# A gate convolution in PSUM, operands in small steps, one tile in another pool and a last column set after loading: several edits to a hybrid transformer block

## The chip, the cores and the metric

The kernel runs on one core of one Trainium2 chip. Its engines are TensorE (PE, matrix products), VectorE (DVE), ScalarE (ACT), GpSimd (POOL) and SyncE (SP, which here only issues loads); each works through its own queue in order. The metric is the device time of one execution, in microseconds (us); lower is better.

## The reference

A block of a generator over 2048 tokens of width 1024 (and 256 context tokens) is computed in fp32. After three kinds of heads (neighbourhood attention, a gating MLP, a convolution module) come an output projection, a residual, and the part that matters here, a gated MLP with a centred depthwise convolution of three tokens on its gate, 2816 channels wide:

```python
x = x + gate1 * (mix @ w_out)                      # output projection, residual
h = modulate(rmsnorm(x), shift2, scale2)           # mean square over the 1024 channels
g, u = split(h @ w_up)                             # gate and up, 2816 each
a = silu(dwconv3(g, ffn_conv_w, ffn_conv_b)) * u   # over tokens t-1, t, t+1
x = x + gate2 * (a @ w_down)
out = rmsnorm(x)
```

## The kernel before, in words

Tokens are kept in four blocks of 512 (0 to 3), a tile is 128 channels x 512 tokens. PE multiplies with fp32 split in two: ACT writes a high half (a copy rounded to fp32r), then DVE or POOL writes the low half, source minus high half; three matmuls take the place of one. `halves` and `split_comb` do that for operands, `load_w` for the weights of the projections. Which engine writes the low half of a weight is set by `phase(i)` out of the list `CFG` ("V" DVE, "P" POOL, "PV" both in turn).

**Output projection.** `out_tile(b, f, w)` makes tile f of block b: it loads the old x (`xr`), 24 matmuls go to a PSUM bank `po`, DVE adds the residual (L859, tile `x1`), the result is stored to DRAM as `x1d`, and its squares are summed over f into `accs[b]`, by DVE for blocks 2 and 3 (L310). For block 2 the sum lives in the pool `jp`, in a tile that an earlier stage used; for block 3 it is `ssum_last`. `out_stats` turns a block's sum into the factor `r`, stored as `rsd`.

**Up stage.** The product with `w_up` is done as a 2 x 2 block matrix product with seven products instead of eight: rows are the two halves of the channels, columns two token blocks. Token half t=0 is blocks 0 and 1, t=1 blocks 2 and 3. The seven operands of a half are sums of four tiles b11, b12, b21, b22: T1 = b12 - b11, T2 = b22 - T1, T3 = b22 - b12, T4 = b21 - T2, and B11, B21, B22 as they are. `h2_tile` loads one tile from `x1d`, scales (DVE, L1117) and shifts it (ACT). For t=0 the operands are made at the end of the output projection: `first_half` runs as a second lane in `merge` beside `out_proj`, `first_half_rest` after it; they stay in SBUF in `hcomb`. For t=1 they are made during t=0 by the generator `second_half` and stored to DRAM (`td`), to be read back by `reload`. Each call `next(sh)` performs the code up to the next `yield`.

For each of 11 pairs k, `up_pair(t, k)` calls `winograd` twice, for the gate tiles and the up tiles: seven `up_prod` of 12 matmuls each into the PSUM tiles x, y, z, and sums that DVE makes out of them (L1274 to L1284). The gate goes to `gb` (one buffer), the convolution over it is ACT for the first tap (L1307), DVE for two more (L1309), ACT for silu (L1311), for four tiles; then the products with u (L1314, L1319), the seven combinations for the down stage (POOL) and their stores to `actd`. PE names are `g_5x` (pair 5, gate, PSUM tile x) and `u_5x`.

**Last column.** Pairs of t=0 lack the gate's right neighbour of their last token, which only t=1 has. After t=1, `last_column` computes that column, and it is written into the DRAM tensors `actd[0]` of five products. **Down stage.** `product` loads two tiles at a time (`ra`), splits them (`ah`), builds the weights' halves (`dw`) and multiplies (L1451).

The order of instructions on an engine is set by the planner: by the order of the code, by `merge` and `weave` (lanes weighed by their cost in us), by `high_priority`, and by when pool memory comes free: with `reuse_waits="tile"` a tile waits for whatever last used its addresses.

Of the kernel before, what the change touches and what calls it, by code (L numbers as in the profile page):

```python
# [143 lines left out]
def tile_hybrid_block(ctx: ExitStack, tc: tile.TileContext, a, out):  # L144
# [69 lines left out]
    CFG = "V,P;PV,P;PV,P;PV,P".split(";")  # L214
# [916 lines left out]
    def first_half():  # L1131
# [6 lines left out]
        for kk in range(4):  # L1138
# [12 lines left out]
    def first_half_rest():  # L1151
        for kk in range(4):
            split_comb(B21, kk, held[B21, kk], nc.vector)
        for kk in range(4):
# [2 lines left out]
            nc.gpsimd.tensor_tensor(t2, hh[:, kk, :].bitcast(F32), hl[:, kk, :].bitcast(F32), op=ALU.add)
# [109 lines left out]
    def winograd(w, c12, c21, c22, use_c11, name):  # L1267
# [16 lines left out]
        nc.vector.tensor_tensor(c12, c12, z, op=ALU.add)  # L1284

    def up_pair(t, k, wg, wu):
        nm = f"{t}_{k}"
# [16 lines left out]
        for i, l in ((0, 0), (1, 1), (1, 0), (0, 1)):
            f, o = k + NP * i, l * TB
            c = stp.tile([P, TB], F32, tag="c", bufs=6, name=f"c{nm}{i}{l}")
            nc.scalar.activation(c, gb[:, i, o:o + TB], AF.Identity, scale=fcw[:, f, 0:1], bias=fcw[:, f, 3:4])  # L1307
# [41 lines left out]
    for t in range(2):  # L1349
# [256 lines left out]
```

## Time and profile before

| | |
|---|---|
| median of 3 runs | 2421.2 us (2420.14 to 2424.05) |
| the profiled execution | 2424.5 us, span of its records 2422.6 us |
| mean granted PE clock | 0.974 |
| end of attention, start of output projection of blocks 2, 3 | near 975 us |
| up stage, t=0 | from about 1058 to 1505 us |
| up stage, t=1 | from 1505 to 1938 us |
| down stage | from 1938 us to the end |

Rows of a profile give an engine, a line of the kernel, an operation and "out<-in"; numbers of buffers are left out. "[8.89 <-ACT dw000hl L1096]" behind a row means that the engine had been idle for 8.89 us before it, until ACT's instruction of line 1096 that writes `dw000hl` had ended. A busy engine is not at its peak by that alone: the clock column says how fast PE was allowed to run, 1.00 being full speed.

### The profile page before, as it was taken

The page shows a single profiled execution, that of the slowest core. Times are in us where ns is not written, and L with a number is a line of the kernel's source. Part 1 is how long each engine was busy: PE and PEld are TensorE (multiplying, and loading weights), DVE is VectorE, ACT ScalarE, POOL GpSimd, SP SyncE. Part 2 cuts the span into 40 slices and gives each one's busy share as a digit, 9 for nine tenths or more (in the row PEclk, how much of TensorE's full clock was granted, in tenths as well). Part 3 has the DMA queues.
Part 4 walks back from the last instruction along what each step waited for, and adds up shares of the span by engine and source line. Part 5 has one row for each costly group of instructions (what it writes and reads, how often), then busy time and mean ns, then how long its engine had stood idle before and what let it go on. Part 6 is the DMA issues. An engine that isn't in the chain of part 4 may idle for free.

```text
span 2422.6 us, 34336 instructions
## 1 busy us (share of the span) xinstructions
PE 2288.3 (94%) x12452; PEld 1901.2 (78%) x12452; DVE 1841.5 (76%) x2477; ACT 1139.1 (47%) x1988; POOL 1097.0 (45%) x1008
## 2 busy tenths in 40 slices
PE   7999989999998999989999998999999989989996
PEld 5889778988887788768777786888888867868875
DVE  4785656556784974698798888787777768999997
ACT  4765643356565446454343434443443344344443
POOL 0265312012011222455667565556565468665753
PEclk9999999999999999989999999999999999999998
DMA  9675576658878778633334434633233492345322
GB/s 355 232 244 171 201 231 189 179 170 240 246 226 269 197 220 272 221 122 118 126 134 157 152 131 166 234 105 109 96 111 103 135 332 93 93 142 176 96 78 92
DMA packets 186347, 421.74 MB, mean 174 GB/s; under 512 B 27072, under 2 KB 76096, under 8 KB 184128
## 3 DMA queue, kind: packets, MB, share of 16 engines
q1 hardware_dynamic: 144688, 318.82, 42.2%
q0 software_dynamic: 28320, 94.39, 10.4%
q10 hardware_dynamic: 13168, 6.32, 0.9%
q8 instruction: 98, 1.61, 0.3%
q14 instruction: 73, 0.60, 0.1%
HBM read 311.69 MB, written 107.77 MB: 173 GB/s over the span
## 4 chain that ended last, share of the span: by engine, by line
PE 55%; DVE 16%; DMA 12%; issue 7%; ACT 5%; POOL 4%; SPq 1%; DVEq 0%; ACTq 0%; POOLq 0%
PE po L202 4%; PE pv L1451 3%; PE pu L1451 2%; PE pk L202 2%; DMA adaf<-in_ada 2%; PE p L1451 2%; PE obank L202 2%; PE pq L202 2%; PE tp L202 2%; PE s L202 2%; PE tp L208 2%; DMA bias_t<-in_bias 2%; DVE cv L573 1%; DMA kk<-ks 1%; DMA xb<-x1d 1%
## 5 line engine op out<-in xcount | busy, mean ns | idle before, releaser
L573 DVE SCALAR_TENSOR_TENSOR cv<-hconv,cst,cv 128x512 f32<-128x512 f32 x240 | 213.9, 933 | 12.3 <-ACT cv L567 12.2
L693 DVE CUSTOM_DVE_ANT_0 sb<-s,bias_t 128x544 f32<-128x544 f32 (+3 forms) x128 | 105.0, 821 | 107.7 <-PE s L202 82.6
L696 ACT ACTIVATE sb<-sb,mx 128x544 f32<-128x544 f32 (+3 forms) x128 | 106.3, 831 | 167.7 <-DVE mx L693 163.2
L1309 DVE SCALAR_TENSOR_TENSOR c<-gb,cst,c 128x512 f32<-128x512 f32 x176 | 166.1, 968 | 3.1 <-ACT c L1307 2.8
L1096 ACT ACTIVATE ah<-ra 128x512 fp32r<-128x512 f32 x154 | 95.0, 623 | 119.8 <-PE pu L1451 32.6
L1097 POOL TENSOR_TENSOR ah<-ra,ah 128x512 fp32r<-128x512 f32 x72 | 112.0, 1569 | 69.4 <-ACT ah L1096 69.4
L202 PE MATMUL s<-kk,qq 128*128 128x256 f32 (+4 forms) x512 | 103.6, 325 | 14.5 <-DMA kk<-ks 8.4
L202 PEld LDWEIGHTS s<-kk,qq 128*128 128x128 f32 x512 | 89.4, 193 | 34.0 <-issue 12.5
L208 PE MATMUL tp<-cst,sb 128*128 128x128 f32 (+2 forms) x672 | 98.4, 277 | 11.4 <-DVE pt L728 7.6
L208 PEld LDWEIGHTS tp<-cst,sb 128*128 128x128 f32 (+2 forms) x672 | 80.6, 140 | 31.2 <-DVE pt L728 8.9
L1097 DVE TENSOR_TENSOR ah<-ra,ah 128x512 fp32r<-128x512 f32 x82 | 84.3, 1030 | 19.0 <-ACT ah L1096 19.0
L1307 ACT ACTIVATE c<-gb,cst 128x512 f32<-128x512 f32 x88 | 69.0, 809 | 27.7 <-DVE gb L1282 26.2
L962 POOL TENSOR_TENSOR adaf<-adaf,adaf 128x1024 f32<-128x1024 f32 x16 | 40.9, 2559 | 89.7 <-ACT adaf L959 89.7
L1311 ACT ACTIVATE c<-c 128x512 f32<-128x512 f32 x88 | 55.3, 629 | 52.5 <-DVE c L1309 52.2
L726 ACT ACTIVATE pt<-tp 128x384 f32<-128x384 f32 (+2 forms) x128 | 61.2, 478 | 36.3 <-PE tp L208 35.9
L728 DVE COPY pt<-tp 128x256 f32<-128x256 f32 (+1 forms) x128 | 57.7, 450 | 24.5 <-PE tp L208 24.2
L959 ACT ACTIVATE adaf<-adaf,silu_c 128x256 f32<-128x256 f32 x128 | 54.3, 498 | 43.2 <-DMA adaf<-in_ada 42.6
L196 POOL DMA_DIRECT2D actd<-c x66 | 36.5, 553 | 80.6 <-DVE c L1319 64.2
L196 POOL DMA_DIRECT2D x1d<-x x30 | 16.6, 553 | 117.3 <-DVE x L859 89.3
L196 POOL DMA_DIRECT2D ks<-k x60 | 33.5, 561 | 77.7 <-ACT k L226 47.5
L196 POOL DMA_DIRECT2D mixd<-att x14 | 7.7, 550 | 134.2 <-DVE att L227 130.3
L202 PE MATMUL obank<-pt,vt 128*64 128x128 f32 (+2 forms) x832 | 58.4, 277 | 0.2 <-DVE pt L728 0.2
(2410 smaller groups left out, 8022.3 us busy)
## 6 DMA issues: line engine op xcount, KB each, us to landing
ra<-actd SPq DMA_DIRECT2D x70, 512.0 KB
wg<-in_w_up SPq DMA_DIRECT2D x44, 512.0 KB
wu<-in_w_up SPq DMA_DIRECT2D x44, 512.0 KB
actd<-tt POOLq DMA_DIRECT2D x88, 256.0 KB, 2.4
actd<-c POOLq DMA_DIRECT2D x66, 256.0 KB, 2.4
adaf<-in_ada SPq DMA_DIRECT2D x32, 512.0 KB
qq<-qs SPq DMA_DIRECT2D x64, 256.0 KB
adaf<-in_ada SPq DMA_DIRECT2D x8, 1024.0 KB
```

What stands on the lines that cost most here:

```text
L196: st_eng[0].dma_start(plain(dst), plain(src))
L202: x = nc.tensor.matmul(*args, **kw)
L208: x = nc.tensor.transpose(*args)
L573: nc.vector.scalar_tensor_tensor(acc[ct], hb[:, ct, k:k + TB], cvw[:, ct, k:k + 1], acc[ct], op0=ALU.mult, op1=ALU.add)
L693: x = nc.vector.tensor_tensor_reduce(out=sb[:, w], in0=s[:, w], in1=bt[:, w], scale=-1.0, scalar=3.0e38, op0=ALU.add, op1=ALU.min, accum_o ...
L696: nc.scalar.activation(sb[:, w], sb[:, w], AF.Exp, bias=mx, scale=-1.0, accum_out=rs[:, cb, j:j + 1])
L726: nc.scalar.activation(dst, src, AF.Copy)
L1096: nc.scalar.activation(hl[:, 0, :], src, AF.Copy)
L1097: eng.tensor_tensor(hl[:, 1, :], src, hl[:, 0, :].bitcast(F32), op=ALU.subtract)
L1307: nc.scalar.activation(c, gb[:, i, o:o + TB], AF.Identity, scale=fcw[:, f, 0:1], bias=fcw[:, f, 3:4])
L1309: nc.vector.scalar_tensor_tensor(c, gb[:, i, o + d:o + d + TB], fcw[:, f, d:d + 1], c, op0=ALU.mult, op1=ALU.add)
L1451: nc.tensor.matmul(ps[i], w[:, ww, sl], ah[:, aa, :], start=start and k_ == 0 and m == 0, stop=(k_ == NP - 1 and m == 2), skip_group_check ...
```

## The change

Six edits.

1. `phase(2)` with "V,P" is set ahead of the last `merge`, so DVE alone writes the low halves of the last projection weights (six of them go from POOL to DVE).
2. The sum of squares of block 2 (`ssum_2`) lies in the pool `pair` instead of `jp`.
3. In `first_half` and `first_half_rest` the low halves of B11 and B22 and the additions `td` go from POOL to DVE (12 operations of 128x512).
4. `second_half` makes its operands in seven steps for each kk, with all subtractions and splits on DVE (8 splits were POOL's), and is called by `step` at two places of each `winograd` of t=0 from the second pair on; `run_all(sh)` performs what is left.
5. For t=0 the first tap and the first DVE tap of the convolution go to a PSUM tile (`cs`, one buffer, tag "st"), the second DVE tap reads it and writes `c` in SBUF.
6. The five DMAs of the last column go; instead ACT copies the column into each loaded `ra` tile of the five products (30 copies of 128x2 or 128x1) ahead of the split.

```diff
-    CFG = "V,P;PV,P;PV,P;PV,P".split(";")
+    CFG = "V,P;PV,P;V,P".split(";")
...
+        elif b == 2 and f == 0:
+            pair("skip")
+            accs[b] = pairp.tile([P, 2, TB], F32, tag="pair", name="ssum_2")[:, 0, :]
+            nc.scalar.activation(accs[b], x1, AF.Square)
...
-                split_comb(p, kk, x, nc.gpsimd if p == B11 else nc.vector)
+                split_comb(p, kk, x, nc.vector)
...
-            nc.gpsimd.tensor_tensor(t2, hh[:, kk, :].bitcast(F32), hl[:, kk, :].bitcast(F32), op=ALU.add)
+            nc.vector.tensor_tensor(t2, hh[:, kk, :].bitcast(F32), hl[:, kk, :].bitcast(F32), op=ALU.add)
...
-            split_comb(B22, kk, h2_tile(0, kk, 1, 1, held["rs"], "xe"), nc.gpsimd)
+            split_comb(B22, kk, h2_tile(0, kk, 1, 1, held["rs"], "xe"), nc.vector)
...
+    phase(2)
...
+        def out_(p, kk, x, eng):
+            if p in SPLIT:
+                x = halves(x, fws, "sp", 3, f"tbs{kk}{p}", eng)
+            store(td[p][:, kk], x)
+
+        def less(kk, x, y, n):
+            t = tt(f"tb{kk}{n}")
+            nc.vector.tensor_tensor(t, x, y, op=ALU.subtract)
+            return t
+
         for kk in range(4):
-            xs = []
-            for i in range(2):
-                xs += [h2_tile(1, kk, i, l, rs, "xb") for l in range(2)]
-                yield
-            cs = combine(*xs, f"tb{kk}", nc.vector)
-            for p in range(7):
-                c = cs[p]
-                if p in SPLIT:
-                    c = halves(c, fws, "sp", 3, f"tbs{kk}{p}", nc.vector if p < 3 else nc.gpsimd)
-                store(td[p][:, kk], c)
-                if p == 3:
-                    yield
+            b11, b12 = (tile(kk, 0, l) for l in range(2))
+            yield
+            t1 = less(kk, b12, b11, 0)
+            store(td[B11][:, kk], b11)
+            b22 = tile(kk, 1, 1)
+            yield
+            out_(T1, kk, t1, nc.vector)
+            t3 = less(kk, b22, b12, 2)
+            yield
+            t2 = less(kk, b22, t1, 1)
+            store(td[B22][:, kk], b22)
+            out_(T3, kk, t3, nc.vector)
+            yield
+            b21 = tile(kk, 1, 0)
+            out_(T2, kk, t2, nc.vector)
+            yield
+            t4 = less(kk, b21, t2, 3)
+            store(td[B21][:, kk], b21)
+            yield
+            out_(T4, kk, t4, nc.vector)
             yield
...
         nc.vector.tensor_tensor(c22, c22, z, op=ALU.add)
+        step()
         up_prod(B21, x, w, False)
...
         nc.vector.tensor_tensor(c12, c12, z, op=ALU.add)
+        step()
...
+        def step():
+            if t == 0 and k > 0:
+                next(sh, None)
...
-        if t == 0:
-            next(sh, None)
...
-            nc.scalar.activation(c, gb[:, i, o:o + TB], AF.Identity, scale=fcw[:, f, 0:1], bias=fcw[:, f, 3:4])
-            for d in (1, 2):
-                nc.vector.scalar_tensor_tensor(c, gb[:, i, o + d:o + d + TB], fcw[:, f, d:d + 1], c,
+            ps = c if t else pp.tile([P, TB], F32, tag="st", bufs=1, name=f"cs{nm}{i}{l}")
+            nc.scalar.activation(ps, gb[:, i, o:o + TB], AF.Identity, scale=fcw[:, f, 0:1], bias=fcw[:, f, 3:4])
+            for d, to in ((1, ps), (2, c)):
+                nc.vector.scalar_tensor_tensor(to, gb[:, i, o + d:o + d + TB], fcw[:, f, d:d + 1], ps,
                                                op0=ALU.mult, op1=ALU.add)
...
-        for p, v in ((T2, t2), (T1, t1), (T3, t3), (T4, b12), (B22, b22)):
-            nc.scalar.dma_start(actd[0][p][:, :, TB - 1:], v.unsqueeze(2))
+        lastc.update({T2: t2, T1: t1, T3: t3, T4: b12, B22: b22})
...
-            if t == 0 and k > 0:
-                next(sh, None)
         if t == 0:
+            run_all(sh)
             reload()
...
+                        if t == 0 and p in lastc:
+                            nc.scalar.activation(at[:, 0:n, TB - 1:], lastc[p][:, k:k + n].unsqueeze(2), AF.Copy)
```

How the rows move, at three places. Line numbers of the changed kernel are 4 to 36 higher for the same statement; numbers behind a name tell buffers apart.

DVE before, at the end of block 3's output projection: the rows with `po` are the residual adds of its last two tiles, `xa`, `xc` and `xe` are tiles of the operands of t=0, `hl` low halves, `td` the tile T4.

```order
L859 SCALAR_TENSOR_TENSOR x_10690<-po_10665,modv,xr_10663 128x512
L1117 SCALAR_TENSOR_TENSOR xc_10711<-xc_10711,a_115,r_10253 128x512
L1127 TENSOR_TENSOR hl_0_10119<-xa_10528,hh_0_10118 128x512
L1117 SCALAR_TENSOR_TENSOR xc_10739<-xc_10739,a_115,r_10253 128x512
L1158 TENSOR_TENSOR td_10838<-xc_10644,td_10838 128x512
L310 TENSOR_TENSOR ssum_last<-ssum_last,sqn_10693 128x512
L1117 SCALAR_TENSOR_TENSOR xe_10853<-xe_10853,a_115,r_10255 128x512
L1158 TENSOR_TENSOR td_10843<-xc_10711,td_10843 128x512
L859 SCALAR_TENSOR_TENSOR x_10733<-po_10704,modv,xr_10702 128x512
L1158 TENSOR_TENSOR td_10848<-xc_10739,td_10848 128x512
L1117 SCALAR_TENSOR_TENSOR xe_10859<-xe_10859,a_115,r_10255 128x512
L1274 TENSOR_TENSOR gb<-g_0p_10882,g_0y 128x512
```

And DVE at the same place now:

```order
L859 SCALAR_TENSOR_TENSOR x_10691<-po_10666,modv,xr_10664 128x512
L310 TENSOR_TENSOR ssum_last<-ssum_last,sqn_10655 128x512
L1161 TENSOR_TENSOR td_10849<-hh_0_10119,hl_0_10120 128x512
L1121 SCALAR_TENSOR_TENSOR xe_10860<-xe_10860,a_115,r_10256 128x512
L310 TENSOR_TENSOR ssum_last<-ssum_last,sqn_10694 128x512
L1162 TENSOR_TENSOR td_10849<-xc_10740,td_10849 128x512
L859 SCALAR_TENSOR_TENSOR x_10734<-po_10705,modv,xr_10703 128x512
L1301 TENSOR_TENSOR gb<-g_0p_10883,g_0y 128x512
L1131 TENSOR_TENSOR hl_0_10825<-xe_10854,hh_0_10824 128x512
L1131 TENSOR_TENSOR hl_0_10825<-xe_10860,hh_0_10824 128x512
L310 TENSOR_TENSOR ssum_last<-ssum_last,sqn_10737 128x512
```

The halves of `xa` and the scalings of `xc` now stand further ahead; five rows instead of seven lie between the last two residual adds, and the last row of `ssum_last`, which stood five rows behind the last add, stands four behind it, ahead of any of the up stage's weight splits. The first scaling of `xa` stood behind block 3's second residual add and now stands right behind that of block 2's sixth tile.

DVE before, around pair 5's gate in token half 0: `tb` and `tbs` are block work of `second_half`, `wu_5hl` and `wg_6hl` weight splits, `gb` the gate sums, `c_500` a conv tile.

```order
L1309 SCALAR_TENSOR_TENSOR c_500_12609<-gb,cst,c_500_12609 128x512
L1097 TENSOR_TENSOR wg_6hl_12766<-wg_60_12754,wg_6hl_12766 128x512
L1107 TENSOR_TENSOR tb_12556<-xb_12420,tb_12555 128x512
L1108 TENSOR_TENSOR tb_12557<-xb_12420,xb_12242 128x512
L1097 TENSOR_TENSOR tbs_12564<-tb_12556,tbs_12564 128x512
L1097 TENSOR_TENSOR tbs_12568<-tb_12555,tbs_12568 128x512
L1109 TENSOR_TENSOR tb_12558<-xb_12416,tb_12556 128x512
L1282 TENSOR_TENSOR gb<-g_5p_12462,g_5y 128x512
L1097 TENSOR_TENSOR wu_5hl_12600<-wu_50_12576,wu_5hl_12600 128x512
L1309 SCALAR_TENSOR_TENSOR c_511_12614<-gb,cst,c_511_12614 128x512
L1309 SCALAR_TENSOR_TENSOR c_510_12619<-gb,cst,c_510_12619 128x512
```

And DVE now, from the sum (L1310) that follows that gate's product T4 on; `cs` is the PSUM tile:

```order
L1310 TENSOR_TENSOR gb<-g_5p_12506,g_5y 128x512
L1101 TENSOR_TENSOR wu_5hl_12635<-wu_50_12611,wu_5hl_12635 128x512
L1301 TENSOR_TENSOR u<-u_5p_12671,u_5y 128x512
L1312 TENSOR_TENSOR gb<-gb,g_5z 128x512
L1101 TENSOR_TENSOR wg_6hl_12815<-wg_6s_12805,wg_6hl_12815 128x512
L1101 TENSOR_TENSOR wu_5hl_12638<-wu_51_12612,wu_5hl_12638 128x512
L1343 SCALAR_TENSOR_TENSOR c_500_12644<-gb,cst,cs_500_12645 128x512
L1101 TENSOR_TENSOR wu_5hl_12641<-wu_5s_12618,wu_5hl_12641 128x512
L1343 SCALAR_TENSOR_TENSOR cs_511_12651<-gb,cst,cs_511_12651 128x512
L1343 SCALAR_TENSOR_TENSOR c_511_12650<-gb,cst,cs_511_12651 128x512
L1304 TENSOR_TENSOR u<-u_5p_12671,u_5y 128x512
L1343 SCALAR_TENSOR_TENSOR cs_510_12657<-gb,cst,cs_510_12657 128x512
```

The run of five rows of block work ahead of the gate sum is gone; before it now stand single rows of block work, further up. One conv tile is finished before the next begins: `cs_511` comes after the second row of `c_500`, `cs_510` after that of `c_511`.

ACT before, at the end of the up stage:

```order
L1311 ACTIVATE c_1000_17547<-c_1000_17547 128x512
L1342 DMA actd_103<-pc 1408x1x1
L1311 ACTIVATE c_1001_17562<-c_1001_17562 128x512
L1342 DMA actd_99<-pc 1408x1x1
L1342 DMA actd_98<-pc 1408x1x1
L1342 DMA actd_100<-pc 1408x1x1
L1342 DMA actd_102<-pc 1408x1x1
L1096 ACTIVATE ah_17785<-ra_17783 128x512
L1096 ACTIVATE dw000hl<-wd_17754 128x512
```

And ACT there now:

```order
L1345 ACTIVATE c_1000_17592<-c_1000_17592 128x512
L1345 ACTIVATE c_1001_17607<-c_1001_17607 128x512
L1100 ACTIVATE dw000hl<-wd_17794 128x512
L1100 ACTIVATE dw001hl<-wd_17794 128x512
L1100 ACTIVATE dw002hl<-wd_17794 128x512
L1100 ACTIVATE dw003hl<-wd_17794 128x512
L1100 ACTIVATE dw004hl<-wd_17795 128x512
L1100 ACTIVATE dw005hl<-wd_17795 128x512
L1100 ACTIVATE ah_17825<-ra_17823 128x512
```

The five DMAs of 1408 single elements each are gone from ACT's queue, and six weight halves of the first product now stand ahead of its first operand's.

More of the change, by code (lines that the diff above doesn't have):

```diff
@@ L1204, in second_half, with tile @@
         yield
-        for kk in range(4):
-            xs = []
-            for i in range(2):
-                xs += [h2_tile(1, kk, i, l, rs, "xb") for l in range(2)]
-                yield
-            cs = combine(*xs, f"tb{kk}", nc.vector)
-            for p in range(7):
-                c = cs[p]
-                if p in SPLIT:
-                    c = halves(c, fws, "sp", 3, f"tbs{kk}{p}", nc.vector if p < 3 else nc.gpsimd)
-                store(td[p][:, kk], c)
-                if p == 3:
-                    yield
+        def tile(kk, i, l):
+            return h2_tile(1, kk, i, l, rs, "xb")
+        def out_(p, kk, x, eng):
[6 more added lines that the diff above has]
+            return t
+        for kk in range(4):
+            b11, b12 = (tile(kk, 0, l) for l in range(2))
[18 more added lines that the diff above has]
+            out_(T4, kk, t4, nc.vector)
             yield
@@ L1265, in up_prod, with winograd @@
                 start = False
-    def winograd(w, c12, c21, c22, use_c11, name):
+    def winograd(w, c12, c21, c22, use_c11, name, step):
         x, y, z = (pp.tile([P, TB], F32, tag=t, bufs=b, name=name + t) for t, b in (("x", 3), ("y", 2), ("z", 2)))
@@ L1294, in up_pair @@
         winograd(w, gb[:, 0, 1 + TB:1 + 2 * TB], gb[:, 1, 1:1 + TB], gb[:, 1, 1 + TB:1 + 2 * TB],
-                 lambda x: nc.scalar.activation(gb[:, 0, 1:1 + TB], x, AF.Copy), "g" + nm)
+                 lambda x: nc.scalar.activation(gb[:, 0, 1:1 + TB], x, AF.Copy), "g" + nm, step)
         if t == 0:
@@ L1313, in up_pair @@
         winograd(w, u[:, 0, :], u[:, 1, :], u[:, 2, :],
-                 lambda x: nc.vector.tensor_tensor(cc[0, 0], cc[0, 0], x, op=ALU.mult), "u" + nm)
+                 lambda x: nc.vector.tensor_tensor(cc[0, 0], cc[0, 0], x, op=ALU.mult), "u" + nm, step)
         if t == 0:
@@ L1325, in up_pair @@
             store(actd[t][p][:, k, :], cs[p])
+    lastc = {}
     def last_column():
```

## The prediction

> **What bounds it now.** I read the page first, then the waits of PE, then stretches of the span, then single stalls. The page's first line says who is close to its limit; the two ACT groups are needed below.
>
> ```profile
> PE 2288.3 (94%) x12452; PEld 1901.2 (78%) x12452; DVE 1841.5 (76%) x2477; ACT 1139.1 (47%) x1988; POOL 1097.0 (45%) x1008
> ...
> L1307 ACT ACTIVATE c<-gb,cst 128x512 f32<-128x512 f32 x88 | 69.0, 809 | 27.7 <-DVE gb L1282 26.2
> ...
> L1311 ACT ACTIVATE c<-c 128x512 f32<-128x512 f32 x88 | 55.3, 629 | 52.5 <-DVE c L1309 52.2
> ```
>
> PE is busy for 2288.3 of 2422.6 us, so what a change that removes no matmul can give is PE's idle time and the time in which its clock is low. The waits of PE (total, times, longest) show which idle time lies where the diff reaches:
>
> ```profile
> PE p L1451 <- ACT dw000hl L1096: 8.9, 1, 8.9
> ...
> PE po L202 <- DVE x L859: 7.4, 2, 4.2
> ...
> PE u_9x L1263 <- ACT u_9p L1272: 5.2, 1, 5.2
> PE u_7x L1263 <- ACT u_7p L1272: 4.1, 1, 4.1
> PE u_5x L1263 <- ACT u_5p L1272: 4.0, 1, 4.0
> PE u_3x L1263 <- ACT u_3p L1272: 4.0, 1, 4.0
> ```
>
> Three places: the end of the output projection (po), the up stage's token half 0 (u_3 to u_9), and the first product of the down stage (p). Each stall also lowers the clock after it, so I price each from windows. Columns: PE busy, PE loads, DVE, ACT, POOL, PE clock, DMA share, GB/s.
>
> ```profile
> 1025.00:1075.00 50.00, 38.86 (x135) 29.71 (x135) 49.10 (x56) 27.98 (x45) 25.41 (x19) 0.83 0.45 153
> ...
> 1045.00:1050.00 5.00, 1.93 (x9) 1.28 (x7) 5.00 (x5) 1.31 (x2) 2.62 (x3) 0.94 0.01 5
> 1050.00:1055.00 5.00, 4.81 (x11) 3.79 (x12) 5.00 (x10) 3.15 (x6) 0.56 (x1) 0.50 0.66 210
> ```
>
> From 1025 to 1075 PE idles 50 − 38.86 = 11.1 us, and its 38.86 busy at a clock of 0.83 lose another 0.17 × 38.86 = 6.6: 17.7 us in all. DVE is busy for 49.10 of the 50: here DVE is the bound. The next rows are six of the up stage's pairs (14 products of 12 matmuls each):
>
> ```profile
> 1110.26:1148.34 38.08, 38.08 (x176) 31.73 (x175) 29.54 (x37) 18.41 (x29) 23.79 (x26) 1.00 0.35 118
> ...
> 1186.45:1230.69 44.24, 40.13 (x167) 32.05 (x167) 37.96 (x43) 18.52 (x31) 28.25 (x34) 0.96 0.47 173
> 1230.69:1268.79 38.10, 38.10 (x170) 31.56 (x169) 33.94 (x39) 16.09 (x27) 24.52 (x27) 1.00 0.31 111
> 1268.79:1314.04 45.25, 41.23 (x169) 33.50 (x169) 39.30 (x45) 18.52 (x31) 30.13 (x35) 0.92 0.49 173
> ...
> 1352.12:1396.88 44.76, 40.63 (x169) 32.46 (x169) 38.75 (x45) 18.52 (x31) 29.59 (x35) 0.96 0.49 170
> ...
> 1434.97:1481.35 46.38, 41.18 (x169) 33.50 (x169) 38.12 (x44) 18.51 (x31) 31.22 (x34) 0.93 0.47 165
> ```
>
> A pair without trouble is 38.1 us of pure PE, and DVE needs 29.5 to 34 of it. Every second pair loses 6.15, 7.16, 6.67 and 8.29: 28.3 us. One such stall by rows of DVE, POOL and ACT:
>
> ```profile
> 1289.25 3.98 DVE L1109 TENSOR_TENSOR tb<-xb,tb 128x512 f32<-128x512 f32 x1
> 1293.16 0.67 DVE L1282 TENSOR_TENSOR gb<-g_5p,g_5y 128x512 f32<-128x512 f32 x1
> ...
> 1289.58 1.30 POOL L1097 TENSOR_TENSOR tbs<-tb,tbs 128x512 fp32r<-128x512 f32 x1
> ...
> 1291.39 1.28 POOL L1249 TENSOR_TENSOR wg_6s<-wg_6s,wg 128x512 f32<-128x512 f32 x1
> ...
> 1293.87 1.52 ACT L1307 ACTIVATE c<-gb,cst 128x512 f32<-128x512 f32 x2 [4.29 <-DVE gb L1282]
> 1295.29 0.57 ACT L1272 ACTIVATE u_5p<-u_5x 128x512 f32<-128x512 f32 x1
> ```
>
> The last subtraction of the block's burst (L1109) lasts 3.98 us instead of some 0.7, over two POOL tensor operations. The gate sum (L1282) queues behind it on DVE, ACT's conv taps wait for that, and the copy u_5p that frees PE's bank queues behind the taps.
>
> **The change, part by part.**
>
> *Gate conv in PSUM, small steps (up stage).* The rows for their prices:
>
> ```profile
> DVE xb L1117 <- DMA xb<-x1d: 22.7, 8, 4.0
> ...
> L1309 DVE SCALAR_TENSOR_TENSOR c<-gb,cst,c x176: 733/743/4225, 1087.1 to 1930.2; 128x512 f32<-128x512 f32 x176
> ...
> L1117 DVE SCALAR_TENSOR_TENSOR xb<-xb,a,r 128x512 f32<-128x512 f32 x16 | 17.4, 1089 | 22.7 <-DMA xb<-x1d 22.7
> ...
> L1309 DVE SCALAR_TENSOR_TENSOR c<-gb,cst,c 128x512 f32<-128x512 f32 x73 | 62.3, 877 | 1.4 <-ACT c L1307 1.3
> ```
>
> The first row sums DVE's waits for loads of xb; the second gives the conv's shortest and median time in both token halves, the fourth its 73 between 1100 and 1500. Now each group of products takes seven steps, a step at two places of every winograd, so that no run of five block operations stands ahead of a gate sum. DVE per pair: 29.5 in the first pair row is a pair that carries no block work. Its 8 conv operations have a mean of 0.877; the gate sums, which read PSUM, keep 0.67 beside POOL in the stall above, so the conv with an operand in PSUM should keep its shortest 0.733. That is 8 × 0.144 = 1.1 less: 28.4. The 48 block operations (16 scalings, 16 subtractions, 16 splits, 8 of which were POOL's) over eight pairs are 6 per pair, 6.5 at the scaling's 1.09.
>
> One PSUM bank for four conv tiles adds a wait: a tile's first tap on ACT comes after the second DVE operation of the tile ahead, and on ACT also behind that tile's silu, so 0.63 + 0.81 = 1.44 lie between them. Behind the waiting operation on DVE are weight splits and the sums of the up part. In the new order other rows stand in two of the four gaps; in the other two stands one row of 0.7 or none, so about 0.9 is left of each: 1.8 per pair. Sum 36.7, and up to 2 for loads of xb that land late (the four waits that made up most of 22.7 above were 4.0 each in a burst; the loads now come by one or two and some queue on SP behind weight loads of the next pair). So 37 to 39 of 38.1: nearly full, but even. The row 1230.69 shows DVE at 33.9 losing nothing, the rows at 38 to 39 with a burst losing 6 to 8. The gain's ends are therefore 28.3 (all stalls go) and 0 (pairs that are bound by DVE lose as much); I take 17, which leaves about 1 us in each of the ten pairs behind the first, nearer to the upper end since no row in the new order blocks as long as 3.98. POOL loses eight splits of 1.3 and keeps its stores; their number is the same, now one or two at a time. The last steps end with pair 8, so what runs the rest of them at the end of the half finds nothing.
>
> [...]
>
> *Sum of squares in another pool, low halves and splits on DVE (output projection).*
>
> ```profile
> 986.23 0.75 DVE L859 SCALAR_TENSOR_TENSOR x<-po,modv,xr 128x512 f32<-128x512 f32 x1 [0.87 <-PE po L202]
> ...
> 1017.26 2.78 DVE L1117 SCALAR_TENSOR_TENSOR xa<-xa,a,r 128x512 f32<-128x512 f32 x4 [5.43 <-DMA xa<-x1d]
> ...
> 1043.81 4.37 DVE L1117 SCALAR_TENSOR_TENSOR xa<-xa,a,r 128x512 f32<-128x512 f32 x1
> ...
> 1065.05 0.74 DVE L859 SCALAR_TENSOR_TENSOR x<-po,modv,xr 128x512 f32<-128x512 f32 x1
> ...
> 1071.46 1.67 ACT L1126 ACTIVATE hh<-xc 128x512 fp32r<-128x512 f32 x3 [1.47 <-DVE ssum_last L310]
> ...
> L250 DVE TENSOR_TENSOR wo36l<-wo36s,wo36h 128x1024 fp32r<-128x1024 f32 x1 | 1.2, 1207 | 0.0
> ...
> L250 POOL TENSOR_TENSOR wo35l<-wo35s,wo35h 128x1024 fp32r<-128x1024 f32 x1 | 2.9, 2920 | 2.2 <-ACT wo35h L247 2.2
> ...
> L1157 POOL TENSOR_TENSOR td<-hh,hl 128x512 f32<-128x512 f32 x4 | 7.7, 1942 | 7.9 <-DVE hl L1127 7.9
> ```
>
> Block 2's sum of squares held memory that the up stage's operands need, so their loads waited for its end: DVE first scales one (xa) at 1017.26, after 5.43 of waiting. In the new order that row stands behind the residual add of block 2's sixth tile, which ran at 986.23: 30 us earlier. That is between five and six output tiles, of 24 matmuls or 24 × 38.08/168 = 5.44 us each.
>
> Moved to DVE are 6 low halves at 1.21 and 12 operations at 0.68 (the clean price of a 128x512 subtraction): 15.4. Gone from POOL are the same: 6 at 2.4 to 2.9, 8 at 1.3 and 4 at 1.94, 33 us in which a DVE operation could be caught, as at 1043.81, where 4.37 stands for 0.74. If half of that was felt, DVE's total is level; that is my middle. What is gained is where the work stands. From 986 to 1025 DVE has idle time (the 5.43 alone is more than the two stalls at L859, 7.4 together, need in slack), so the rows that came between two residual adds at 1030 and 1049 have already run. At the end the last square sum stands behind three rows of 0.7 after the last residual add, and that add behind five rows instead of seven after the one before. Before, the add came at 1065.05 and the ACT halves (L1126) that wait for the sum's memory at 1071.46; with rows of 0.7 they would come some 3.5 behind the add. Of 17.7 lost I take 13: both stalls at L859 with half of their low clock (7.4 + 3.3) and part of the rest. The ends are 0 (the 15.4 are felt and no block was) and 17.7.
>
> On SP the early loads pass two residual tiles and three weight loads; each is awaited a tile later, so I price that at nothing. The cover is the one tile of 5.44; a load that lands late there would cost PE at most what it is late.
>
> *Last column in loaded tiles (down stage).*
>
> ```profile
> 1931.61 14.62 ACTq L1342 DMA_DIRECT2D actd<-pc  x4
> ...
> 1946.28 0.63 ACT L1096 ACTIVATE ah<-ra 128x512 fp32r<-128x512 f32 x1 [14.71 <-DMA wd<-in_w_down]
> ...
> 1947.48 4.41 PE L1451 MATMUL p<-ah,dw000hl 128*128 128x512 f32 x12 [8.89 <-ACT dw000hl L1096]
> ...
> L1333 ACT ACTIVATE g<-g x1: 213/213/213, 1927.0 to 1927.0; 128x22 f32<-128x22 f32 x1
> ```
>
> ACT's queue issues four element-wise DMAs for 14.62 us, and the first halves of the down stage stand behind them. That the page names wd as releaser is not the cause: the queue was occupied until 1946.2. Without them the halves can start as u_10 ends; PE's 8.89 goes, and the low clock of the first 12 matmuls (4.41 against 12 × 38.08/168 = 2.72) goes with it: 10.6, of which I take 10 (0 if the first loads of ra land late, 11 at most). The 30 copies, of 128x2 and 128x1, at the 0.21 of the nearest row are 6.3 us of ACT in five products of this half. A copy stands between the landing of a tile and its split; four such tiles are in flight and ACT is busy 47% of the span, so I price it at nothing. Without that cover it is 6.3.
>
> **Sum.** 17 + 13 + 10 = 40. Against the profiled execution's 2424.5 that is 2384.5; the median of the runs shown is 2421.2, 3.3 lower, so 2381 for a median, and I say 2382.
>
> **Rivals.**
> *All goes.* The dips vanish whole (28.3), the projection gives 16, the down stage 11: 55, so 2366. For it speaks that DVE's 33.9 costs nothing; against, that DVE's estimate reaches past 38.1.
> *DVE becomes the bound of token half 0.* Pairs settle at 40.9, the mean of the ten pairs now (38.1 + 28.3/10), and this part gains 0: 2421 − 23 = 2398. DVE's upper estimate of 39 speaks for it.
> *The early start is no use.* The moved 15.4 are all felt and DVE stays the projection's bound: 17 + 10 = 27, so 2394. For it speaks 49.10 of 50 busy.
> *Slower.* The conv chain on one bank serialises DVE, ACT and PE: each of four tiles waits its 1.44 and behind one POOL operation of 1.3 that blocks the row ahead, 11 us per pair instead of 1.8. There is one gate buffer, so the next pair's sums wait for the end of the chain, and PE with them. DVE's pair is then 28.4 + 6.5 + 11 = 45.9, 7.8 over PE's 38.1: 78 over ten pairs, less the 28.3 now lost and the 23 of the other parts, 27 slower: 2448. It decides from 43.2 per pair (28.3 + 23 over ten pairs). Against it: two of the four gaps hold other work.
>
> **How the numbers follow.** Chances: forecast 0.52 (its own range 2374 to 2391), all goes 0.15, DVE the bound 0.18, no use of the early start 0.07, slower 0.08. Of "DVE the bound" I put 0.03, where its pairs pass 41, and of "slower" 0.01 within 0.2%; 0.2%, 4.8 us, is about what a measurement of this kernel can tell from no change. So faster 0.89, same 0.04, slower 0.07. The range 2362 to 2408 leaves out the slower case, the worse third of "DVE the bound" and the far end of "all goes".
>
> **What would show it.** Right: no wait u_3x to u_9x on ACT above 1 us and pairs of 38 to 40 us; the first xa near 986 and no window near 1050 with half a clock; ACT's first halves of the down stage before 1940 of the old scale, with no queue time of 14 us. Wrong: all pairs of token half 0 alike at 41 or more with DVE over 95% busy; PE waits on L859 as long as before; a new wait on ra in front of the first p.

## The result and the profile after

The changed kernel took 2385.98 us (median of 4 runs, 2378.94 to 2388.35), the kernel before 2420.7 (median of 4 runs): 34.7 us less by the medians. The ratio on record is 0.9849, 95% interval 0.9826 to 0.9872; it is not the quotient of the two medians, which is 0.9857. Run again beside other kernels it gave 0.9858 (0.9845 to 0.987). The forecast was 2382, range 2362 to 2408.

The page of the profiled execution (2384.91 us) begins so; the second row is the convolution of token half 1, still in SBUF:

```profile
PE 2268.9 (95%) x12452; PEld 1890.4 (79%) x12452; DVE 1818.5 (76%) x2503; ACT 1140.8 (48%) x2018; POOL 1045.1 (44%) x982
...
L1343 DVE SCALAR_TENSOR_TENSOR c<-gb,cst,c 128x512 f32<-128x512 f32 x88 | 97.5, 1131 | 1.5 <-ACT c L1341 1.3
```

PE's waits: the first row is of the kernel before, the others are of the changed one. The three places of before (L859, u_3x to u_9x, dw000hl) are gone from the list; what stands there now is new or has grown (g_0y only from 3.2 to 3.9):

```profile
PE fms L1477 <- DVE sq L1472: 7.4, 3, 3.0
...
PE fms L1513 <- DVE sq L1508: 9.7, 3, 5.4
...
PE g_0y L1290 <- DMA hh<-td: 3.9, 2, 2.8
...
PE g_2y L1290 <- DVE gb L1304: 3.4, 1, 3.4
...
PE g_5y L1290 <- DVE gb L1304: 2.9, 1, 2.9
...
PE g_6y L1290 <- DVE gb L1304: 1.9, 1, 1.9
```

To see where the 34.7 us came from I compare the times of the same PE instruction in several profiles. Until tile 3 of block 2 PE's order is the same, and yet that tile ends between 968.9 and 977.2 in the profiles of this study: the stages ahead scatter by some 8 us from run to run. So each time below, in us, is counted from that tile's end and set against the kernel before (minus is earlier). "Last po" is the last matmul of the output projection, "up 0" the last matmul of product tile u_0z, "up 10" and "t=1" that of u_10z in the two token halves, "p" the first matmul of the down stage. Each row is one profile.

| kernel | last po | up 0 | up 10 | t=1 | p | end |
|---|---|---|---|---|---|---|
| changed | -8.3 | -14.3 | -33.3 | -29.9 | -39.0 | -34.2 |
| the same, another run | -8.2 | -12.4 | -30.1 | -28.3 | -37.4 | -31.8 |
| edit 6 alone | -1.8 | -0.4 | 0.0 | -0.8 | -9.9 | -5.5 |
| edits 1, 2, 3 | -8.0 | -14.0 | -15.5 | -14.8 | -14.9 | -14.9 |
| edit 2 alone | +2.3 | -1.6 | -5.4 | -4.5 | -4.6 | -4.2 |
| edits 1, 3 | -12.3 | -4.8 | -5.0 | -4.0 | -3.8 | -3.9 |
| edit 4 alone | -3.6 | -0.8 | -9.7 | -10.5 | -10.9 | -11.0 |
| edit 5 alone | -3.5 | +0.1 | -18.6 | -15.0 | -18.7 | -17.5 |
| all but 4 | -8.9 | -14.7 | -33.2 | -32.4 | -41.5 | -36.4 |
| all but 5 | -8.4 | -12.6 | -27.8 | -26.8 | -35.8 | -31.1 |
| changed, copies on POOL | -8.9 | -14.7 | -29.8 | -30.6 | -39.6 | -42.2 |
| all but 4, copies on POOL | -8.0 | -12.4 | -27.7 | -27.0 | -36.1 | -38.0 |

The changed kernel gains 14.3 us until the first pair, 19.0 in the rest of token half 0, gives back 3.4 in token half 1, gains 9.1 at the head of the down stage, and gives back 4.8 inside it. The first, second and fourth of these were in the forecast's sum (13, 17, 10); the two losses were not. The 3.4 are lost by the end of pair 1 of token half 1. Longer waits account for about half of them: those for td, the row g_0y above, came to 3.2 before already and are now 3.9, and a wait of 1.1 for a weight half (g_1x) is new. The rest is not accounted for.

**The projection.** The window from 1025 to 1075 again, then the one that answers to it in the work: the last po ends at 1045.0 in this profile and at 1058.7 before, so it lies 13.7 earlier.

```profile
1025.00:1075.00 50.00, 48.37 (x212) 39.35 (x212) 44.81 (x67) 29.34 (x48) 15.60 (x13) 1.00 0.37 127
1011.30:1061.30 50.00, 48.37 (x217) 39.47 (x216) 46.93 (x71) 31.85 (x51) 8.76 (x12) 1.00 0.53 182
```

In the second, PE is busy for 48.37 of 50 at full clock (38.86 at 0.83 before), and DVE runs 71 instructions in 46.93 us where it ran 56 in 49.10: 0.66 us each instead of 0.88. POOL's busy time there fell from 25.41 to 8.76. The first xa now starts at 982.53, behind block 2's sixth tile as forecast.

**Token half 0.** The convolution by groups of DVE rows between 1080 and 1480, and the forms of one line with shortest, median and longest time:

```profile
L1343 DVE SCALAR_TENSOR_TENSOR cs<-gb,cst,cs 128x512 f32<-128x512 f32 x41 | 30.7, 749 | 11.6 <-ACT cs L1341 11.4
L1343 DVE SCALAR_TENSOR_TENSOR c<-gb,cst,cs 128x512 f32<-128x512 f32 x40 | 29.6, 740 | 0.3
...
L1121 DVE SCALAR_TENSOR_TENSOR xb<-xb,a,r 128x512 f32<-128x512 f32 x16 | 19.2, 1202 | 4.2 <-DMA actd<-c 3.1 <-DMA xb<-x1d 1.1
```
```profile
L1343 DVE SCALAR_TENSOR_TENSOR c<-gb,cst,c x88: 734/746/4219, 1518.5 to 1894.7; 128x512 f32<-128x512 f32 x88
L1343 DVE SCALAR_TENSOR_TENSOR cs<-gb,cst,cs x44: 739/750/758, 1064.8 to 1477.9; 128x512 f32<-128x512 f32 x44
L1343 DVE SCALAR_TENSOR_TENSOR c<-gb,cst,cs x44: 731/740/750, 1069.7 to 1480.5; 128x512 f32<-128x512 f32 x44
```

With one operand in PSUM none of 88 operations lasted over 0.758 us; the 88 of token half 1, with both in SBUF, reach 4.219, and each of the 20 of them over 1 us ran beside a tensor operation of POOL (before, 25 of 176 took over 1 us, each beside one as well). The price of the single bank is the wait for ACT's first tap, 11.4 us over some ten pairs, 1.1 a pair. Four pairs as windows, the second to the sixth without the fourth:

```profile
1123.18:1170.35 47.17, 43.79 (x180) 35.61 (x180) 40.48 (x51) 20.76 (x36) 26.37 (x33) 0.93 0.46 156
1170.35:1208.21 37.86, 37.86 (x169) 31.36 (x168) 33.66 (x42) 17.81 (x30) 24.89 (x29) 1.00 0.40 143
...
1245.83:1287.75 41.92, 39.06 (x173) 32.03 (x172) 38.53 (x48) 19.82 (x34) 27.40 (x34) 1.00 0.44 151
1287.75:1327.78 40.03, 38.14 (x168) 31.26 (x168) 36.32 (x46) 18.63 (x31) 25.01 (x31) 1.00 0.49 171
```

The pairs are not even. The second takes 47.17 (the first, which ends early, 34.75), with PE's wait of 3.4 at g_2y and a clock of 0.93; the ten behind pair 0 take 395.7 together, 39.6 each, where they took 414.8 before. The stall in the fifth pair, the row of 41.92, in DVE's and POOL's rows:

```profile
1260.01 1.78 DVE L1221 TENSOR_TENSOR tb<-xb,xb 128x512 f32<-128x512 f32 x1
1261.71 0.74 DVE L1343 SCALAR_TENSOR_TENSOR cs<-gb,cst,cs 128x512 f32<-128x512 f32 x1
1262.48 1.65 DVE L1101 TENSOR_TENSOR tbs<-tb,tbs 128x512 fp32r<-128x512 f32 x1
1264.06 0.67 DVE L1304 TENSOR_TENSOR gb<-g_5p,g_5y 128x512 f32<-128x512 f32 x1
...
1262.30 1.27 POOL L1278 TENSOR_TENSOR wu_5s<-wu,wu_5s 128x512 f32<-128x512 f32 x1
```

A step of block work (tb, tbs) still stands ahead of a gate sum, two operations of 1.7 instead of a burst, and PE's g_5y waits 2.9 us for that sum. Operations as long as the 3.98 us of before have not gone either:

```profile
1182.50 4.19 DVE L1221 TENSOR_TENSOR tb<-xb,tb 128x512 f32<-128x512 f32 x1
...
1295.77 4.02 DVE L1121 SCALAR_TENSOR_TENSOR xb<-xb,a,r 128x512 f32<-128x512 f32 x1
```

PE has no wait behind the first; the second ends some 3 us ahead of PE's wait of 1.9 at g_6y.

**The down stage.** PE's first row there has no wait, and 12 matmuls take 2.88 us (4.41 before):

```profile
1903.01 2.88 PE L1487 MATMUL p<-ah,dw000hl 128*128 128x512 f32 x12
```

Some 200 us later half of the gain is lost again. PE of the kernel before, then ACT, DVE and PE of the changed kernel at the same place:

```profile
2156.89 1.12 PE L1477 MATMUL fms<-sq,cst 128*128 128x512 f32 x2 [2.08 <-DVE sq L1472]
...
2097.72 0.63 ACT L1504 ACTIVATE sq<-x1r 128x512 f32<-128x512 f32 x1 [1.53 <-DVE x1r L1501]
2104.63 0.21 ACT L1472 ACTIVATE ra<-pc 128x2 f32<-128x2 f32 x1 [6.27 <-DMA ra<-actd]
2104.74 0.62 ACT L1504 ACTIVATE sq<-x1r 128x512 f32<-128x512 f32 x1
...
2105.39 0.69 DVE L1508 TENSOR_TENSOR sq<-sq,sq 128x512 f32<-128x512 f32 x1 [4.75 <-ACT sq L1504]
...
2114.99 2.07 PE L1513 MATMUL fms<-sq,cst 128*128 128x512 f32 x2 [5.44 <-DVE sq L1508]
```

A copy of 0.21 us waits 6.27 for its tile to land; the square behind it on ACT's queue waits too, DVE's sum waits for the square, and PE's matmul fms for the sum. PE waited here before too, 2.08 us; now it is 5.44, and the matmuls behind it are slower (the next 11 of pu take 4.95 us, 3.10 before). Against the kernel before, PE is 5.7 us later about ten matmuls behind this row than just ahead of it, and it stays so most of the way to the end.

### The profile page after: what moved, and what is told of

It reads as the page before. It is cut to its first block, busy times and chain, and to the rows that moved or that the text cites. A ratio compares the mean times of both kernels' runs of the same rounds, so it can differ in the third digit from the quotient of the medians.

```text
span 2382.9 us, 34374 instructions
## 1 busy us (share of the span) xinstructions
PE 2268.9 (95%) x12452; PEld 1890.4 (79%) x12452; DVE 1818.5 (76%) x2503; ACT 1140.8 (48%) x2018; POOL 1045.1 (44%) x982
## 3 DMA queue, kind: packets, MB, share of 16 engines
q0 software_dynamic: 28320, 94.39, 10.6%
## 4 chain that ended last, share of the span: by engine, by line
PE 51%; DVE 21%; DMA 12%; issue 8%; ACT 4%; POOL 3%; SPq 1%; DVEq 0%; ACTq 0%; POOLq 0%
DVE cv L573 3%; PE po L202 3%; PE obank L202 3%; PE pu L1487 2%; PE p L1487 2%; PE pq L202 2%; PE s L202 2%; PE tp L208 2%; DVE ah L1101 2%; PE pk L202 2%; PE tp L202 2%; PE pv L1487 2%; DMA bias_t<-in_bias 1%; DMA kk<-ks 1%; POOL ah L1101 1%
## 5 line engine op out<-in xcount | busy, mean ns | idle before, releaser
L573 DVE SCALAR_TENSOR_TENSOR cv<-hconv,cst,cv 128x512 f32<-128x512 f32 x240 | 214.5, 935 | 10.8 <-ACT cv L567 10.6
L202 PE MATMUL s<-kk,qq 128*128 128x256 f32 (+4 forms) x512 | 102.8, 323 | 14.9 <-DVE mx L693 7.5
L202 PEld LDWEIGHTS s<-kk,qq 128*128 128x128 f32 x512 | 88.4, 191 | 34.7 <-DVE mx L693 13.7
L208 PEld LDWEIGHTS tp<-cst,sb 128*128 128x128 f32 (+2 forms) x672 | 80.0, 139 | 32.4 <-DVE pt L728 10.6
L1343 DVE SCALAR_TENSOR_TENSOR c<-gb,cst,c 128x512 f32<-128x512 f32 x88 | 97.5, 1131 | 1.5 <-ACT c L1341 1.3
L1101 DVE TENSOR_TENSOR ah<-ra,ah 128x512 fp32r<-128x512 f32 x82 | 83.9, 1028 | 12.4 <-ACT ah L1100 12.4
L1353 DVE TENSOR_TENSOR c<-c,u 128x512 f32<-128x512 f32 x66 | 52.1, 790 | 0.5
```

Source lines behind the costliest of these rows:

```text
L202: x = nc.tensor.matmul(*args, **kw)
L208: x = nc.tensor.transpose(*args)
L573: nc.vector.scalar_tensor_tensor(acc[ct], hb[:, ct, k:k + TB], cvw[:, ct, k:k + 1], acc[ct], op0=ALU.mult, op1=ALU.add)
L1101: eng.tensor_tensor(hl[:, 1, :], src, hl[:, 0, :].bitcast(F32), op=ALU.subtract)
L1343: nc.vector.scalar_tensor_tensor(to, gb[:, i, o + d:o + d + TB], fcw[:, f, d:d + 1], ps, op0=ALU.mult, op1=ALU.add)
```

## The experiments

Each ratio is to the kernel before on the same chip, with its 95% interval, and the us given beside it are worked out from it; the medians on record differ from that by up to 3 us (edits 1, 2 and 3: 15.4 by the medians, 18 by the ratio). Edits are numbered as in the section on the change.

**Edit 6 alone.**

```diff
-            nc.scalar.dma_start(actd[0][p][:, :, TB - 1:], v.unsqueeze(2))
+                            nc.scalar.activation(at[:, 0:n, TB - 1:], lastc[p][:, k:k + n].unsqueeze(2), AF.Copy)
```

> The kernel before with edit 6 alone (the last column copied into loaded tiles instead of five element-wise DMAs). Theory (ACT's queue held the down stage's first halves back): 9 to 10.6 us faster, the first p of the down stage starts as u_10 ends, and nothing ahead of 1930 us moves. Rival (the wait was for the loads of wd, as the page names them, or the 30 copies cost it back): 0 to 3 us faster, PE still waits 5 us or more ahead of the first p.

Measured: 0.9981 (0.9971 to 0.9992), 4.6 us. Both expectations were half right. The first p comes 9.9 earlier in the table, 9.1 of it behind the end of the up stage, as the theory had it: ACT's queue and not the load of wd held it back. But 4.4 are lost behind it, as the rival had it (the copies cost it back): PE then waits 5.36 for fms, at the same place as in the changed kernel.

**Edits 1, 2 and 3 together, and apart.**

```diff
+            accs[b] = pairp.tile([P, 2, TB], F32, tag="pair", name="ssum_2")[:, 0, :]   # edit 2
...
-                split_comb(p, kk, x, nc.gpsimd if p == B11 else nc.vector)              # edits 1, 3
+                split_comb(p, kk, x, nc.vector)
+    phase(2)
```

> The kernel before with edits 1, 2 and 3 (block 2's sum of squares in another pool, twelve operand operations and six low halves from POOL to DVE). Theory: 13 to 15 us faster, the end of po 13 to 15 us earlier than before relative to the tile ahead of the changed place, no stall on L859 over 2 us. Rival (DVE stays the bound there, the moved 15.4 us are felt): within 3 us of before. A second rival, that part of the 20 us seen by the end of the first pair is scatter of the unchanged stages ahead, would show as an offset already near 980 us.

Measured: 0.9924 (0.991 to 0.9937), 18 us by the ratio, 14.9 by the table, and no wait on L859. The time is the theory's; its place is not, for the last po comes only 8.0 earlier and the rest by the end of the first pair. The second rival holds as well, for a part of the 20 us: in the changed kernel's profile 5.4 of them are there at the tile that ended at 974 before.

> The kernel before with edit 2 alone (only the sum of squares of block 2 in another pool). Theory (the early start is what counts): 8 to 14 us faster, xa near 986, end of po 6 us or more earlier than before against the tile at 974. Rival (POOL's operations still block DVE at the same places, so the moves to DVE carry it): 0 to 5 us faster, a stall of 2 us or more on L859 remains.

Edit 2 alone: 0.9982 (0.9969 to 0.9994), 4 us. The early start as such is not what counts: a wait of 2.7 on L859 remains, as the rival had it, a wait of 4.0 for a sum (n22ms) is new, and the last po comes 2.3 later than before.

> The kernel before with edits 1 and 3 (the moves from POOL to DVE) and without edit 2: the operands still start near 1017. Theory (the collisions with POOL alone set this place): 9 to 15 us faster, as with all three. Rival (both are needed: without the early start the added 15.4 us of DVE stand in its full stretch): 0 to 6 us faster, stalls of PE on L859 remain.

Edits 1 and 3 without edit 2: 0.9988 (0.9976 to 0.9999), 3 us. The gain is in the rival's range; its sign, waits on L859, is not there, for PE's waits have moved behind the projection (below). Neither half brings a third of what they bring together. Edits 1 and 3 were not run apart. A window of each, edit 2 alone first, then edits 1 and 3, then all three:

```profile
1000.00:1025.00 25.00, 19.53 (x82) 15.11 (x81) 24.97 (x27) 15.72 (x26) 10.69 (x10) 0.93 0.67 219
```
```profile
1050.00:1075.00 25.00, 21.38 (x77) 16.70 (x76) 25.00 (x36) 15.98 (x28) 8.99 (x5) 0.81 0.30 100
```
```profile
1025.00:1050.00 25.00, 25.00 (x116) 20.84 (x115) 25.00 (x39) 14.31 (x22) 3.25 (x6) 1.00 0.63 205
1050.00:1075.00 25.00, 23.35 (x103) 18.63 (x102) 21.82 (x32) 14.61 (x26) 9.35 (x7) 1.00 0.28 97
```

With the early start alone DVE is full 25 us sooner and does 27 instructions in that window (0.92 us each, POOL 10.69 busy), so the stall only moves ahead. With the moves alone DVE's operations are quick (40 in the 25 us from 1025 on, 0.63 each), the projection ends 12.3 earlier, but DVE is still full between 1050 and 1075, PE's clock is down to 0.81 there, and PE waits for halves of the operands around the start of that window:

```profile
1048.18 0.50 PE L1264 MATMUL g_0y<-hl,wg_0hl 128*128 128x512 f32 x1 [3.06 <-DVE hl L1127]
...
1061.32 0.79 PE L1264 MATMUL g_0x<-hl,wg_0hl 128*128 128x512 f32 x1 [2.39 <-DVE hl L1127]
```

With all three DVE is full from 1000 to 1050 at short operations (39 in 25 us, 0.64 each), and no longer so after 1050.

**Edit 4 alone, edit 5 alone.**

```diff
+            yield                                    # edit 4: seven steps for each kk, all on DVE
+        step()
...
+            ps = c if t else pp.tile([P, TB], F32, tag="st", bufs=1, name=f"cs{nm}{i}{l}")   # edit 5
```

> The kernel before with edit 4 alone (second half's operands in seven small steps, all on DVE). Theory A (the burst of block work is what stalls every second pair): 10 to 18 us faster, the stalls u_3x to u_9x gone although the convolution still collides with POOL. Theory B (the convolution's collisions with POOL are what makes DVE late): 0 to 6 us faster, pairs that all lose 2 to 3 us.

Edit 4: 0.996 (0.9947 to 0.9972), 9.7 us: below theory A's range by a hair and above theory B's. Four of the ten pairs still take 41.8 to 43.7, against 44.2 to 46.4 before in every second one (two windows, an easy pair and the worst):

```profile
1186.80:1226.60 39.80, 38.08 (x167) 30.86 (x166) 35.44 (x43) 17.02 (x29) 23.02 (x28) 1.00 0.44 153
1226.60:1270.30 43.70, 41.09 (x172) 33.05 (x171) 38.79 (x47) 19.17 (x32) 28.80 (x34) 0.96 0.49 165
```

> The kernel before with edit 5 alone (convolution of token half 0 accumulated in one PSUM tile). Theory A (the burst stalls the pairs): 0 to 6 us faster, stalls of 3 to 4 us at every second pair remain, and DVE waits for ACT's first taps some 1 us per pair. Theory B (the collisions of the convolution do): 10 to 18 us faster, stalls gone. Rival on the other side (the single bank serialises the chain): slower by 5 us or more, with DVE waits on L1307 above 3 us per pair.

Edit 5: 0.9926 (0.9913 to 0.9939), 17.9 us, all of it in token half 0 (18.6 in the table). That is theory B's figure, and PE's longest wait there is 2.0 us. DVE's wait for the first tap, the mechanism of the third expectation, is there and small:

```profile
DVE cs L1311 <- ACT cs L1309: 13.8, 13, 1.4
```

But theory B's cause, the convolution's own collisions with POOL, is not shown by this. Two more things changed beside it: the last subtraction of the burst, and what stands ahead of the copy u_5p on ACT. The first row is of the kernel before, the others are of this run:

```profile
L1109 DVE TENSOR_TENSOR tb<-xb,tb x4: 3970/3981/3983, 1206.5 to 1456.6; 128x512 f32<-128x512 f32 x4
...
L1109 DVE TENSOR_TENSOR tb<-xb,tb x4: 678/1550/2424, 1210.8 to 1444.8; 128x512 f32<-128x512 f32 x4
...
1290.98 0.60 ACT L1272 ACTIVATE u_5p<-u_5x 128x512 f32<-128x512 f32 x1 [0.64 <-DVE gb L1282]
```

The bursts stand ahead of the gate sums as before, but their last subtraction, 3.98 us in each of the four stalls, now takes 2.42 at most; and ACT makes u_5p right behind the gate sum, where two conv taps stood ahead of it.

**The changed kernel without one of the two.**

> The changed kernel without edit 4 (second half's operands made in bursts again, with POOL's eight splits). Theory from the single edits (the convolution in PSUM alone brings the whole gain of token half 0; small steps add nothing to it): within 4 us of the changed kernel. Rival (steps and PSUM both needed, as the forecast summed them): 8 us or more slower than the changed kernel.

Without edit 4: 0.9853 (0.9838 to 0.9868), as the theory had it. Not to be told from the changed kernel (0.9849 and 0.9858): beside the PSUM tile the small steps add nothing that these runs can show.

> The changed kernel without edit 5 (convolution of token half 0 in SBUF again). Theory (collisions with POOL stretch DVE; steps alone brought 10): 5 to 10 us slower than the changed kernel, 25 to 30 faster than before. Rival (the small steps carry the gain in the presence of the others): within 3 us of the changed kernel.

Without edit 5: 0.9859 (0.9844 to 0.9873). Here the theory failed: I expected 5 to 10 us more than the changed kernel, and it is the same within the intervals (the table has it 1 to 3 us behind). Beside the other edits either of the two is enough for most of the gain, though alone one brought 9.7 and the other 17.9. The convolution's operations are in this run no shorter than before:

```profile
L1341 DVE SCALAR_TENSOR_TENSOR c<-gb,cst,c 128x512 f32<-128x512 f32 x81 | 76.0, 962 | 2.0 <-ACT c L1339 2.0
```

A mean of 0.962, where it was 0.87, and yet the pairs of token half 0 are quick: long operations of the convolution alone did not cause the stalls. What is gone here too is the long subtraction: none of tb takes over 1.90. With edit 4 alone two of them took 3.59, one ahead of the wait at u_4x (2.6) and one ahead of that at u_6x (1.9).

**The copies on POOL.**

```diff
-                            nc.scalar.activation(at[:, 0:n, TB - 1:], lastc[p][:, k:k + n].unsqueeze(2), AF.Copy)
+                            nc.gpsimd.tensor_copy(at[:, 0:n, TB - 1:], lastc[p][:, k:k + n].unsqueeze(2))
```

> The changed kernel with the 30 copies of the last column on POOL instead of ACT. Theory (a copy that waits for its load holds back ACT's squares behind it, DVE's sums and PE's matmul fms): the stall of 5.4 us at fms goes and the kernel is 3 to 5 us faster than the changed one. Rival (POOL's queue holds its low halves back in the same way, or the stall at fms is DVE's own lateness): no faster, a wait of PE on ah or fms of 3 us or more in the same product.

Measured: 0.9823 (0.9808 to 0.9837), which is 6 to 8 us better than the changed kernel's two ratios and more than the 3 to 5 of the theory. The wait at this fms is gone, the 2.08 of before with it, and from p to the end the kernel needs 2.6 us less than before, where the changed one needs 4.8 more. ACT at the same place now waits for DVE alone:

```profile
2100.13 0.61 ACT L1100 ACTIVATE dw052hl<-wd 128x512 fp32r<-128x512 f32 x1
2104.47 0.63 ACT L1504 ACTIVATE sq<-x1r 128x512 f32<-128x512 f32 x1 [3.73 <-DVE x1r L1501]
```

POOL waits for late tiles as well, 7.0 us in all instead of ACT's 49.7:

```profile
L1472 POOL COPY ra<-pc x30: 179/646/657, 1958.5 to 2117.6; 128x2 f32<-128x2 f32 x25, 128x1 f32<-128x1 f32 x5
...
  DMA ra<-actd: 7.0, 8
```

**The two together, beside the changed kernel on one chip.** The first is the changed kernel, the second the same without edit 4 and with the copies on POOL (the two diffs above).

> The changed kernel once more, beside the next one on the same chip: 34 to 38 us faster than before, with the stall of 5 us at fms.

> The changed kernel without edit 4 and with the last column's copies on POOL. Theory (small steps bring nothing beside the convolution in PSUM, the copies on ACT cost 4 to 5 us): 3 to 8 us faster than the changed kernel. Rival (steps help the start of token half 1): no faster than the changed kernel with copies on POOL, some 2380 us.

Measured: the changed kernel 2389.74 us, 0.9858 (0.9845 to 0.987), with the same 5.4 at fms; without edit 4 and with copies on POOL 2381.0, 0.9818 (0.9805 to 0.9832). The intervals do not touch: 8.7 us faster than the changed kernel, the fastest of the study, though not to be told from the version that keeps edit 4 (0.9823). So it is a little more than the theory's 3 to 8, and the rival's time, some 2380, holds too: this run does not decide whether edit 4 helps. In the table the version with edit 4 is ahead by 4.2 with the copies on POOL and behind by 2 to 5 with them on ACT.

## Why the prediction was right, and where it was not

- **The sum.** 17 + 13 + 10 = 40 stood against the profiled execution; the two profiles differ by 39.7. But 5.5 of these are scatter of the unchanged stages ahead, so the change itself is worth 34, as the medians say; that the profiles differ by 40 is luck. The sum came out 6 too high: two losses that it did not have, 4.8 inside the down stage and 3.4 in token half 1, are partly made up by 3.3 more than forecast in its first two terms, and the head of the down stage gave 0.9 less. That the forecast of 2382 came within 4 us rests in part on these errors going opposite ways.
- **The copies of the last column, priced at nothing: the step that failed.** The cover named was that four tiles are in flight and ACT is busy 47%. Neither helped: the tile has four buffers and ACT is busy 48%, but what was not asked is what stands behind a copy on ACT's queue while it waits for its load. A square of the final norm does, once. Between p and the end this cost 4.4 to 5.6 us, net of 1.5 that the quicker first matmuls gain, in each of the kernels that have the copies on ACT (edit 6 alone, the changed one twice, all but 4, all but 5), and nothing where POOL makes them. The row used for its price gave 0.21 us, which was right; the wait of 6.27 ahead of it was left out.
- **The head of the down stage.** 10 forecast (10.6 before rounding down), 9.1 measured up to the first matmul, and its first 12 matmuls take 2.88 instead of 4.41: 10.6 together. That wd was not the cause, as the forecast read against the page's releaser, is shown by edit 6 alone, whose first p comes 9.1 earlier behind the end of the up stage with the loads of wd as they were.
- **The projection.** 13 forecast, 12.4 and 14.3 measured. The reason given was the early start, with the moves to DVE as level. The runs show that it needs both: 4 for the early start, 3 for the moves, 15 for the two together. The forecast's rival "the early start is no use", in which DVE stays full, describes rather the kernel with edits 1 and 3 alone.
- **Token half 0.** 17 forecast, 19.0 and 17.7 measured from the first pair to the last, of which 1.8 to 3.4 are given back in token half 1. The size is right, the picture behind it only in part. Conv operations: forecast at 0.733 each, measured 0.740 and 0.749. Bubbles of the single bank: 1.8 a pair forecast, 1.1 measured. Block work: 6.5 a pair forecast; its scaling came at 1.20 instead of 1.09, and all 48 operations took 58 us, 7.3 a pair over eight pairs. DVE's sum of 37 to 39 a pair was still on the high side: the mean of the ten is 33.5, the three busiest of those shown have 40.5, 38.5 and 36.3. "Nearly full, but even" failed: the pairs run from 34.8 to 47.2, and "no row in the new order blocks as long as 3.98" failed with the rows of 4.19 and 4.02. New waits on the gate sum (3.4, 2.9, 1.9) are the loss that was left in the sum, in three pairs instead of 1 us in each of ten. Of the signs named, no wait u_3x to u_9x above 1 us came true and pairs of 38 to 40 did not.
- **What brings the gain there** was not told apart by the forecast, which put steps and PSUM into one term. The PSUM tile alone gives it, and so, beside the other edits, do the steps without it.
- **The price of a PSUM operand.** The forecast took the conv's shortest time, 0.733, because gate sums keep 0.67 beside POOL. In the stall it named, POOL's last operation ends at 1292.67 and the sum starts at 1293.16, so that row does not show it. The other sums do: in the kernel before, 22 of the 44 of L1282 ran beside a tensor operation of POOL, 14 of them from start to end, and none took over 0.689. The conv bears it out: 46 of its 88 operations with one operand in PSUM ran beside POOL's tensor operations, none over 0.758. Nor does reading PSUM cost anything that shows here: medians of 0.750 and 0.740 against 0.746 with both operands in SBUF, and in the kernel before 0.746 for the residual add from PSUM (L859) against 0.743 for the conv in SBUF.
- **The slower rival** needed 43.2 us a pair. Its wait appeared at 1.1 a pair, and the ten pairs took 39.6 on average.

What stays open: why edits 4 and 5 replace each other beside the projection's edits, when alone they bring 9.7 and 17.9. What the rows show is that with either one the subtraction of 3.98 us no longer stands ahead of a gate sum (2.42 at most with edit 5 alone, 1.90 in all but 5). That this is the cause, and not DVE's slack or the order of ACT's taps, is a guess that no run tested: none held the order fixed and moved only the operand.

## What to carry to other kernels

Before a small operation on an in-order queue is priced by its own duration, write down what it waits for and what stands behind it: a 0.21 us copy that waited for a load cost 5 us, and the same copy on another queue cost none. Where DVE and POOL were both busy, an operand in PSUM kept a DVE operation short here (0.758 us at the longest instead of 4.2), but test whether those are the operations that hurt: here the stalls went without it too. Try edits together as well as alone: earlier start and fewer collisions brought 4 and 3 us apart and 15 together, small steps and the PSUM tile 9.7 and 17.9 apart and, beside the others, no more than the larger one. Compare stages from a landmark behind the last unchanged instruction, since the unchanged part alone differed by 8 us between profiles.

## What the runs showed of the hardware that was not expected

POOL takes 0.65 us (median of 30, 0.18 to 0.66) for a copy of 128x2 or 128x1 for which ACT takes 0.205; it was still the better place. The same instructions ahead of the change end between 968.9 and 977.2 us in profiles of kernels that share them.
